# Two 32-row groups and held-back stores in a streaming RMSNorm + SiLU kernel

## The chip, the cores and the metric

The kernel runs on one core of one Trainium2 chip. The metric is the device time of one launch in microseconds. Before the change it is 160.66 us, the median of three runs that lie between 160.58 and 160.77 us. One further execution was taken with the hardware profiler: its own time was 160.9 us, and the span from its first to its last instruction was 159.4 us. The core has four engines that matter here (DVE, ACT, POOL and PE, the last of which only passes signals on), SP, whose queue issues the transfers, and 16 DMA engines that move the bytes between HBM and SBUF.

## The reference

```python
batch, seq, dim = 16, 1024, 512
x     = np.random.randn(batch, seq, dim).astype(np.float32)
gamma = np.ones(dim, dtype=np.float32)
eps   = np.float32(1e-5)

rms    = np.sqrt(np.mean(x ** 2, axis=-1, keepdims=True) + eps)
x_norm = x / rms * gamma
out    = x_norm * (1.0 / (1.0 + np.exp(-x_norm)))
```

There are 16,384 rows of 512 floats. Each row is normalised by its own root mean square, scaled by gamma and passed through SiLU. Every input byte is read once and every output byte is written once: 33.55 MB each way.

## The kernel before, in words

**Tiling.** Each of the 128 partitions of SBUF handles 128 rows ("rows" from here on means rows of a partition, 0 to 127; one such row is 2 KB for each partition and 256 KB over all of them). `groups` (line 28) says how the rows of a partition lie in HBM: a group of 16 rows covers 128 x 16 consecutive rows of the tensor, and partition p takes 16 consecutive ones of them, which are 32 KB in one piece. `dram` (line 105) turns a piece (first row, count) into that access pattern, and a piece may not cross a group's end. So a transfer of n rows has, for each partition, one contiguous run of n x 2 KB on both sides.

**The buffer.** `xb` holds `ring` = 96 rows a partition. Rows 96 to 127 reuse the places of rows 0 to 31, so those loads must wait until the stores of rows 0 to 31 have landed.

**The transfers.** `loads` and `stores` (lines 30 to 33) list the pieces, and `order` (lines 34 to 37) is the order in which SP issues them: eight loads (rows 0 to 95), then three stores (rows 0 to 31), then three loads (rows 96 to 127), then seven stores (rows 32 to 127). The first two loads are moved ahead of the start barrier (`early` = 2, lines 138 to 149). `load` (line 121) waits on the semaphore `st[u]` of a store whose place it overwrites; `store` (line 132) waits on `s_swish`, which counts finished units of compute. All of these transfers are on the one queue of SP, and SP works through them strictly in that order: a transfer that waits holds back everything listed behind it.

**The compute.** Work goes in units of `cn` = 4 rows, 32 units in all. PE waits for each load and adds its units to `s_land` (lines 156 to 159). ACT squares the four rows of a unit (`square`, line 184), DVE sums two of them (`sums`, line 211), POOL makes 1/sqrt (`power`, line 165), DVE multiplies each row by it and by gamma (`norm`, line 220), and ACT applies SiLU in place (`swish`, line 196) and counts `s_swish` up. ACT squares a unit two units before it applies SiLU (`lead` = 2).

Of the kernel before, what the change touches and what calls it, by code (L numbers as in the profile page):

```python
# [9 lines left out]
def kernel(  # L10
# [7 lines left out]
    nc = tc.nc  # L18
# [6 lines left out]
    of = out.flatten_outer_dims()  # L25
    R, D = xf.shape

    groups = [16] * 8
    ring = 96
    loads = [(0, 4), (4, 4), (8, 8), (16, 16), (32, 16), (48, 16), (64, 16), (80, 16)]  # L30
    loads += [(96, 16), (112, 8), (120, 8)]
    stores = [(0, 16), (16, 8), (24, 8), (32, 16), (48, 16), (64, 16), (80, 16)]
    stores += [(96, 16), (112, 8), (120, 8)]
    order = [("load", i) for i in range(loads.index((96, 16)))]
    order += [("store", t) for t in range(3)]
    order += [("load", i) for i in range(loads.index((96, 16)), len(loads))]
    order += [("store", t) for t in range(3, len(stores))]
    early = 2
    cn = 4
    n_sq = 2  # L40
# [46 lines left out]
    ld = [nc.alloc_semaphore(f"ld{t}") for t in range(len(loads))]  # L87
# [14 lines left out]
    def need(ins, sem, value):  # L102
        return ins.wait_op(sem, value, "sem-ge")

    def dram(ap, piece):
        a, n = piece
        g = max(g for g in range(len(groups)) if first[g] <= a)
        r = a - first[g]
        assert r + n <= groups[g], piece
        rows = ap[P * first[g] : P * (first[g] + groups[g])]  # L110
        return rows.rearrange("(p n) d -> p n d", n=groups[g])[:, r : r + n, :]

    def buf(piece):
        a, n = piece
        at = a % ring
        assert at + n <= ring, piece
        return xb[:, at : at + n, :]
# [3 lines left out]
    def load(i):  # L121
        a, n = loads[i]
        for u, (c, m) in enumerate(stores):
            over = c + ring < a + n and a < c + m + ring
            if over and u not in stored_by_sync:
                nc.sync.wait_ge(st[u], 16)
                stored_by_sync.add(u)
        return nc.sync.dma_start(
            out=buf(loads[i]), in_=dram(xf, loads[i])
        ).then_inc(ld[i], 16)  # L130

    def store(t):
        need(
            nc.sync.dma_start(out=dram(of, stores[t]), in_=buf(stores[t])),
            s_swish, ends[t],
        ).then_inc(st[t], 16)
# [11 lines left out]
        )  # L148
        entry.insert(at, ins)
    for what, t in order[early:]:  # L150
        load(t) if what == "load" else store(t)

    def take(queue, sem, n):
        need(queue.nop(nofuse=True), sem, n).then_inc(sem, -n)
# [151 lines left out]
```

## Time and profile before

| | |
|---|---|
| median of three runs | 160.66 us (160.58 to 160.77) |
| the profiled execution: time, span | 160.9 us, 159.4 us |
| ACT, DVE, POOL busy | 129.6, 124.5, 65.4 us |
| HBM read, written | 33.56 MB, 33.55 MB |
| ACT, after its first stalls | busy 99.71 of the 102.55 us from 37.95 to 140.50 us |
| last instruction of DVE, of ACT | about 138.5 and 140.5 us |
| last landing of a store | 159.3 us |

When SP issued each transfer and when its last byte was reported as landed (us from the start of the span, from the issue records and the semaphore updates):

| transfer (first row, rows) | issued | landed |
|---|---|---|
| loads (0,4) (4,4) (8,8) | 0.00, 0.43, 1.92 | 4.76, 7.24, 12.14 |
| loads (16,16) (32,16) (48,16) | 2.29, 2.77, 3.25 | 21.86, 31.57, 41.28 |
| loads (64,16) (80,16) | 3.88, 4.39 | 50.99, 61.62 |
| stores (0,16) (16,8) (24,8) | 30.09, 38.07, 46.05 | 71.29, 76.17, 81.19 |
| loads (96,16) (112,8) (120,8) | 71.31, 76.19, 81.20 | 90.76, 95.66, 100.56 |
| stores (32,16) (48,16) (64,16) | 81.58, 82.05, 93.95 | 110.44, 120.28, 130.15 |
| stores (80,16) (96,16) | 109.92, 125.88 | 139.92, 149.64 |
| stores (112,8) (120,8) | 133.87, 140.49 | 154.48, 159.33 |

Read the second table down its last column: the landings follow one another in the order of issue, and the column has no hole. Where a transfer was issued long before it landed, it stood in line behind the ones above it. From it four stages can be told apart: loads to about 61 us, stores to about 81 us, loads to about 100 us, stores to the end. The page's first two sections give the busy time of the compute engines and, in 40 slices of 4 us, how busy the 16 DMA engines were; its third section gives the number of packets. A packet is one contiguous run that one DMA engine moves: 8 KB for a piece of four rows, 16 KB for eight, 32 KB for sixteen. Each engine serves eight partitions, so it gets eight packets of every transfer, and a 4-byte packet that counts the semaphore up.

### The profile page before, as it was taken

What the parts mean: (1) busy time and instruction counts of PE and PEld (TensorE: products, weight loads), DVE (VectorE), ACT (ScalarE), POOL (GpSimd) and SP (SyncE); (2) the same over time, 40 slices, a digit from 0 to 9 for tenths busy, and PEclk for the clock granted to TensorE, in tenths of its full rate; (3) what the DMA queues carried; (4) which work ended last, traced back from release to release, by engine and by line L of the source; (5) the groups of instructions that cost most, each with busy time, mean ns of one, the idle gap of its engine ahead of it and who ended that gap; (6) DMA issues with size and microseconds to landing.
All of it is one profiled execution on the core that took longest, in us unless ns stands there. A gap on an engine that the chain in (4) does not pass through costs nothing. (4 is left out here: it accounts for less than half of the span.)

```text
span 159.4 us, 900 instructions
## 1 busy us (share of the span) xinstructions
DVE 124.5 (78%) x162; ACT 129.6 (81%) x193; POOL 65.4 (41%) x70
## 2 busy tenths in 40 slices
DVE  0187969999999999999999999999999999700000
ACT  0939959999999999999999999999999995720000
POOL 1052545555555555555555555555555555000000
DMA  7999999999999999999999999999999999999896
GB/s 267 454 465 395 452 469 395 411 502 403 395 469 452 395 395 395 395 399 448 415 448 469 391 432 428 485 428 395 469 444 403 403 493 411 411 469 436 382 419 259
DMA packets 3033, 67.12 MB, mean 421 GB/s; under 512 B 341, under 2 KB 341, under 8 KB 345
## 3 DMA queue, kind: packets, MB, share of 16 engines
q1 hardware_dynamic: 3024, 67.11, 98.8%
q10 hardware_dynamic: 8, 0.01, 0.0%
q14 instruction: 1, 0.00, 0.0%
HBM read 33.56 MB, written 33.55 MB: 421 GB/s over the span
## 5 line engine op out<-in xcount | busy, mean ns | idle before, releaser
L223 DVE SCALAR_TENSOR_TENSOR xb<-xb,rstd,gamma_sb 128x512 f32 (+1 forms) x128 | 87.3, 744 | 0.0
L198 ACT ACTIVATE xb<-xb (+1 forms) x32 | 60.9, 1902 | 2.8 <-DVE xb L223 2.8
L213 DVE TENSOR_REDUCE ms<-sq 128x2 f32<-128x1024 f32 x32 | 39.2, 1224 | 14.0 <-ACT sq L192 10.7
L168 POOL TENSOR_SCALAR aeps<-ms 128x4 f32<-128x4 f32 x32 | 20.6, 644 | 65.6 <-DVE ms L213 65.6
L175 POOL TENSOR_TENSOR rstd<-aeps,neg_half 128x4 f32<-128x4 f32 x32 | 44.1, 1377 | 2.7
L186 ACT ACTIVATE junk<-xb 128x512 f32 (+1 forms) x64 | 38.6, 603 | 4.5 <-PEq L159 4.4
L192 ACT ACTIVATE sq<-xb 128x1024 f32 (+1 forms) x32 | 32.1, 1005 | 0.0
L186 ACT ACTIVATION_READ_ACCUMULATOR junk<-xb 128x1 f32 x64 | 11.9, 186 | 0.0
L206 ACT ACT_TABLE_LOAD x1 | 1.3, 1283 | 3.6 <-issue 3.6
L161 POOL MEMSET gamma<- 128x512 f32 x1 | 0.5, 524 | 1.5 <-POOLq L71 1.5
L233 DVE STREAM_SHUFFLE gamma_sb<-gamma 128x512 f32<-128x512 f32 x1 | 0.7, 721 | 0.0
L287 POOL MEMSET const-float32-0.0<- 128x1 f32 x1 | 0.1, 98 | 0.2 <-issue 0.2
L287 POOL MEMSET const-bfloat16-1.0<- 128x1 bf16 x1 | 0.1, 101 | 0.0
L287 POOL MEMSET const-uint8-127<- 128x1 uint8 x1 | 0.1, 101 | 0.0
L162 POOL MEMSET neg_half<- 128x4 f32 x1 | 0.1, 101 | 0.0
L287 POOL MEMSET const-float32-1.0<- 128x1 f32 x1 | 0.1, 99 | 0.0
L233 DVE LOAD_MASK_SELECT gamma_sb<-gamma x1 | 0.0, 14 | 0.0
## 6 DMA issues: line engine op xcount, KB each, us to landing
xb<-in_x_dram SPq DMA_DIRECT2D x6, 4096.0 KB, 33.4
out_dram<-xb SPq DMA_DIRECT2D x6, 4096.0 KB, 33.1
out_dram<-xb SPq DMA_DIRECT2D x4, 2048.0 KB, 27.9
xb<-in_x_dram SPq DMA_DIRECT2D x3, 2048.0 KB, 19.4
xb<-in_x_dram SPq DMA_DIRECT2D x2, 1024.0 KB, 5.8
gamma<-in_gamma_dram ACTq DMA_DIRECT2D x1, 8.0 KB
```

What stands on the lines that cost most here:

```text
L161: nc.gpsimd.memset(gamma4, 0.0).then_inc(s_zero, 1)
L162: nc.gpsimd.memset(neg_half, -0.5).then_inc(s_half, 1)
L168: nc.gpsimd.tensor_scalar(out=aeps[:, m, :], in0=ms[:, m, :], scalar1=eps_f, scalar2=None, op0=ALU.add,),
L175: nc.gpsimd.tensor_tensor(out=rstd[:, m, :], in0=aeps[:, m, :], in1=neg_half, op=ALU.pow),
L186: acc = nc.scalar.activation(out=junk[(k % turn) * (cn - n_sq) + j - n_sq], in_=rows(at + j, 1)[:, 0, :], func=AF.Square, scale=inv_d**0.5 ...
L192: nc.scalar.activation(out=sq[k % turn], in_=rows(at, n_sq), func=AF.Square, scale=inv_d**0.5,).then_inc(s_sq, 1)
L198: nc.scalar.activation(out=rows(at, cn), in_=rows(at, cn), func=AF.Silu),
L206: nc.scalar.preload_act_table_set("silu_and_others")
L213: nc.vector.tensor_reduce(out=ms[:, k % turn, 0:n_sq], in_=sq[k % turn], op=ALU.add, axis=mybir.AxisListType.X,),
L223: ins = nc.vector.scalar_tensor_tensor(out=row, in0=row, scalar=rstd[:, k % turn, j : j + 1], in1=gamma_sb, op0=ALU.mult, op1=ALU.mult,)
L233: nc.vector.stream_shuffle(gamma_sb, gamma4, [0] * 32), s_gld, 16
L287: nc = _bacc.Bacc("TRN2", target_bir_lowering=False, num_devices=1)
```

## The change

Three things are different. The rows 32 to 63 and 64 to 95 become one group each of 32 rows, so a partition's run in HBM is 64 KB there. The pieces are cut anew: the first loading phase is (0,4) (4,4) (8,8) (16,16) (32,32) (64,28) (92,4), the second (96,16) (112,12) (124,4); the stores are (0,16) (16,16), and later (32,32) (64,32) (96,16) (112,8) (120,8). That makes 10 loads and 7 stores, where there were 11 and 10. And `order` has a third kind of entry, `landed`: ahead of each storing phase SP waits until the next to last load of the phase before has landed, which leaves the last load, four rows, in the queue. The compute code is the same.

```diff
-    groups = [16] * 8
+    groups = [16, 16, 32, 32, 16, 16]
     ring = 96
-    loads = [(0, 4), (4, 4), (8, 8), (16, 16), (32, 16), (48, 16), (64, 16), (80, 16)]
-    loads += [(96, 16), (112, 8), (120, 8)]
-    stores = [(0, 16), (16, 8), (24, 8), (32, 16), (48, 16), (64, 16), (80, 16)]
-    stores += [(96, 16), (112, 8), (120, 8)]
-    order = [("load", i) for i in range(loads.index((96, 16)))]
-    order += [("store", t) for t in range(3)]
-    order += [("load", i) for i in range(loads.index((96, 16)), len(loads))]
-    order += [("store", t) for t in range(3, len(stores))]
+    loads = [(0, 4), (4, 4), (8, 8), (16, 16), (32, 32), (64, 28), (92, 4)]
+    second = len(loads)
+    loads += [(96, 16), (112, 12), (124, 4)]
+    stores = [(0, 16), (16, 16)]
+    storing = len(stores)
+    stores += [(32, 32), (64, 32), (96, 16), (112, 8), (120, 8)]
+    order = [("load", i) for i in range(second)]
+    order += [("landed", loads.index((64, 28)))]
+    order += [("store", t) for t in range(storing)]
+    order += [("load", i) for i in range(second, len(loads))]
+    order += [("landed", loads.index((112, 12)))]
+    order += [("store", t) for t in range(storing, len(stores))]
...
     for what, t in order[early:]:
-        load(t) if what == "load" else store(t)
+        if what == "landed":
+            nc.sync.wait_ge(ld[t], 16)
+        else:
+            load(t) if what == "load" else store(t)
```

## The prediction

> **What bounds the kernel now.** I read the page's first two sections first, then the waits of SP's queue, then the DMA view cut into stretches small enough to hold packets of one size.
>
> ```profile
> span 159.4 us, 900 instructions
> DVE 124.5 (78%) x162; ACT 129.6 (81%) x193; POOL 65.4 (41%) x70
> ...
> DMA  7999999999999999999999999999999999999896
> ...
> q1 hardware_dynamic: 3024, 67.11, 98.8%
> ```
>
> No compute engine is busy for more than 81% of the span, while the 16 DMA engines are at 9 in every slice from the second to the 37th, and q1, SP's queue, has packets in flight for 98.8% of 16 engines' span: 157.5 us for each engine. So the time is the sum of the packets that one DMA engine must move, plus about 1 us until the first packet starts and about half a microsecond from the last to its report. An edit is worth what it does to the number or length of packets, or to a gap between them.
>
> ```profile
> SPq L134 <- ACT xb L198: 97.5, 9, 25.2
> SPq L128 <- DMA out_dram<-xb: 34.1, 3, 24.9
> SPq L270 <- DMA out_dram<-xb: 18.3, 3, 8.7
> ```
>
> SP waits for 97.5 us on compute (L134) and 34.1 us on stores whose places are to be reloaded (L128), yet no DMA slice falls under 9: there is always enough issued ahead. The shortest lead is that of the load of rows 96 on: the store it waits for landed at 71.29, it was issued at 71.31, and two 8-row stores (4.9 us each) were still queued.
>
> Then the packets. In each stretch, share x 16 x length / packets is the mean time of a packet. The four stretches, in order: 63 to 70 us (stores, 32 KB), 57 to 58 and 58 to 60 us (the last two packets of each engine's first loading phase, 32 KB), 96 to 99.4 us (the last loads of the second phase, 16 KB).
>
> ```profile
> DMA packets 96, 3.15 MB, mean 449 GB/s; under 512 B 0, under 2 KB 0, under 8 KB 0
> q1 hardware_dynamic: 96, 3.15, 104.0%
> ...
> DMA packets 16, 0.52 MB, mean 524 GB/s; under 512 B 0, under 2 KB 0, under 8 KB 0
> q1 hardware_dynamic: 16, 0.52, 147.2%
> ...
> DMA packets 16, 0.52 MB, mean 262 GB/s; under 512 B 0, under 2 KB 0, under 8 KB 0
> q1 hardware_dynamic: 16, 0.52, 100.9%
> ...
> DMA packets 92, 1.51 MB, mean 443 GB/s; under 512 B 0, under 2 KB 0, under 8 KB 0
> q1 hardware_dynamic: 92, 1.51, 103.4%
> ```
>
> A 32 KB packet takes 1.0400 x 16 x 7 / 96 = 1.213 us, a 16 KB one 1.034 x 16 x 3.4 / 92 = 0.611 us. But the last two load packets before the first stores take 1.472 and 2.018 us. This is the one place where all engines are slow together: (1.472 - 1.213) + (2.018 - 1.213) = 1.06 us for each engine. Before the second storing phase there is nothing of the kind: 0.611 us is the plain rate.
>
> **The change part by part.**
>
> *Fewer, larger packets.* Each engine gets eight packets of each transfer. Before, 21 transfers are 168 packets and 21 semaphore packets; after, 17 are 136 and 17. A packet's fixed part follows from the two sizes: 1.213 - 0.611 = 0.602 us is 16 KB, so 0.611 - 0.602 = 0.009 to 0.010 us are fixed. One engine's records overlap by 4 ns (32 KB starts stand 1.209 us apart), so 0.005 us is net. Saved: 36 x 0.005 = 0.18 us, at most 36 x 0.010 = 0.36 us. The trace has no 64 KB packet. From the line through 16 and 32 KB it is 2 x 1.204 + 0.010 = 2.417 us; were it split in two, it would cost 2 x 1.213 = 2.426, and the 24 split packets would give 24 x 0.005 = 0.12 back, leaving 0.06 us. I take 0.18, because the line is straight from 8 KB (0.311 us) on. Range of this term: 0 to -0.36 us.
>
> *Rows 32 on arrive later.* ACT squares row 32 at 37.95 us; its 16-row load landed at 31.57. The 32-row load lands with row 63, at about 41.28 as (48,16) did. ACT then stands still for 41.28 - 37.95 = 3.3 us; its chain ends at 143.8 instead of 140.5, since it is busy 99.71 of the remaining 102.55 us and can't catch up. Cover: the last store was issued at 140.49, while the store before it still had the DMA until about 154.0 us. 13 us of lead become 10. Tightest is the new store (64,32), which needs unit 24: ready at 109.92 + 3.3 = 113.3, while (32,32), 19.4 us long from about 100, keeps the engines to about 119. 6 us are left. Rows 64 to 91 land about 58, but ACT wants row 64 at 37.95 + 32 + 3.3 = 73. Cost: nothing; without the cover every microsecond of ACT's delay would count.
>
> *Fewer stores before the reload.* (16,8) and (24,8) become (16,16). The load (112,12) is then issued at about 81 rather than 76 us; ahead of it the load (96,16), 9.7 us, is in the queue. Cost: nothing.
>
> *The two waits.* Behind the waiting SP stand the stores, and behind those, in the first case, the loads from row 96 on, which wait for those stores anyway. At each wait four rows remain queued: 8 x (0.311 - 0.004) = 2.45 us an engine. In that time the semaphore must arrive, SP issue, and the first store packet start. Semaphore: the last 4-byte packet of store (0,16) starts at 70.93 us and its landing is at 71.29: 0.36 us. SP reacts in 0.02 us. From issue to first packet there is one row, the first load into empty engines: issued at 0.00, first packets from 1.02 to 1.55 us. Together 1.40 to 1.93 us, so 0.5 to 1.0 us is left on the slowest engine. The fastest ones are ahead by the spread of the semaphore packets, 0.46 us in the first phase (50.01 to 50.48) and 0.61 in the second (99.46 to 100.07): 0.1 us of hole at worst, on engines that don't end last. Cost: nothing; if the cover fails, the third case below.
>
> By the Trainium skill, page "DMA: Bandwidth & Descriptors", section "Latency and other measured facts", the same wait would be dearer: it gives an HBM access 2 us at high load and a first byte after about 0.6 us, together an estimate of 2.6 us, which is more than the four rows cover. By it each turn would stand dry for some 0.15 us, and the sum below would be about 0.3 us higher; the measured 0.36 us says that this core's queue is not in that state.
>
> *The slow turn at 57 to 61 us.* This decides the sign of anything measurable. Either the 1.06 us stays (bound 0) or the later issue and the 8 KB packets at the turn take it away (bound -1.06). No row shows a turn behind four rows. The nearest row is the second turn, at 100 us: there stores had been queued for 18 us as well (issued at 81.58), and it cost nothing. So early issue by itself is not what costs. What the second turn does not share with the first is that the first brings this run's first writes to the output, and that its load packets are of 32 KB. I take the first reading, a cost of the first stores, and 0.
>
> Sum: -0.18 + 0 + 0 + 0 + 0. On the profiled execution 160.9 (span 159.4 + 1.5) becomes 160.7; that execution stands 0.24 us above the median, so on the median 160.66 - 0.18 = 160.5 us.
>
> **The rivals.**
>
> *The slow turn goes.* For it: the excess falls exactly where stores follow loads, and 16 KB packets show none. Against it: the second turn is free with its stores queued early, and the slow packets come before any store packet has started. 160.48 - 1.06 = 159.4 us; a part of it left, in the ratio of 8 to 32 KB, gives 159.7.
>
> *The engines run dry at the turns.* It decides once the time from issue to first packet exceeds 2.45 - 0.38 = 2.07 us, against 1.02 to 1.55 at the start. Then the engines must be refilled: the 18 packets that start from 1.0 to 1.6 us take 1.263 x 16 x 0.6 / 18 = 0.67 us instead of 0.311, so 0.36 us a turn, and the hole comes on top, 0.48 us if a first packet needs 1 us more than at its slowest. Two turns: 160.48 + 0.72 = 161.2, with holes 162.2 us. For it: the margin is small and nothing shows the latency in a full queue. Against it: both known parts leave 0.5 us.
>
> *64 KB runs are not one packet, or are slower.* 160.6 us when split; a slower rate isn't suggested by any row.
>
> **How the numbers follow.** A measurement of this kernel can tell 0.2%, 0.32 us, from no change: 160.34 to 160.98. Forecast (turn stays, packets saved): 0.44, from 160.3 to 160.7, a quarter of it under 160.34. Turn goes: 0.33, all faster. Dry: 0.18, nearly all slower; larger runs that are slower: 0.05, slower. Faster 0.33 + 0.11 = 0.44, slower 0.23, the rest 0.33. The range goes from 159.2 (turn gone and 0.36 saved) to 161.3 (dry without much of a hole); the forecast's own is 160.3 to 160.7.
>
> **What would show it.** 136 + 17 packets an engine, 2.4 us for 64 KB; ACT idle for some 3 us before row 32 and its end near 144; DMA slices at 9 throughout; and in the stretch before the first stores either packets well above 0.311 and 1.213 us (turn stays) or none. A hole in the DMA row near 61 or 100 us, or a store packet that starts later than 2.07 us after its issue, would make the forecast wrong.

## The result, and the profile after

The changed kernel takes 159.92 us (median of six runs, 159.81 to 159.99) against 160.68 us before (six runs, 160.58 to 160.77). The ratio is 0.9949, with a 95% interval of 0.9939 to 0.9959: 0.76 to 0.82 us less, 0.5%. The profiled execution took 159.97 us with a span of 158.5 us.

The same lines of the page as were shown of before:

```profile
span 158.5 us, 896 instructions
DVE 124.5 (79%) x162; ACT 129.7 (82%) x193; POOL 65.4 (41%) x70
...
DMA  7999997989999969999999999896996996999996
...
q1 hardware_dynamic: 2448, 67.11, 98.6%
```

The compute engines are as busy as they were. There are 2448 packets instead of 3024, which is 16 engines x (136 + 17), and q1 has them in flight for 98.6% of a shorter span: 156.3 us for each engine instead of 157.5. The digits 6 to 8 in the DMA row are not holes. The row counts a packet's whole time in the slice in which it starts, and the packets of 56 and 64 KB take 2.1 and 2.4 us, so the slices of 4 us fill unevenly. By the packet records, an engine is without a packet for less than 0.1 us in all between 2 and 157 us, before and after.

Two stretches of the changed kernel's DMA view, from 57.7 to 59.7 us (the four rows held back ahead of the first stores, 8 KB packets) and from 102 to 116 us (stores of 64 KB runs):

```profile
DMA packets 98, 0.80 MB, mean 401 GB/s; under 512 B 0, under 2 KB 0, under 8 KB 0
q1 hardware_dynamic: 98, 0.80, 96.0%
...
DMA packets 92, 6.03 MB, mean 431 GB/s; under 512 B 0, under 2 KB 0, under 8 KB 0
q1 hardware_dynamic: 92, 6.03, 99.4%
```

By share x 16 x length / packets, the first are 0.960 x 16 x 2.0 / 98 = 0.313 us, the plain time of 8 KB: the slow packets ahead of the first stores are gone. The second are 0.994 x 16 x 14 / 92 = 2.42 us for 64 KB, one packet for each run; their records in the trace stand at 2.418 us.

Where the time went is read best from the landings at the end of each stage (issue plus time to landing, in the trace):

| | before | after | gained so far |
|---|---|---|---|
| rows 0 to 63 loaded | 41.28 | 41.18 | 0.10 |
| rows 0 to 95 loaded | 61.62 | 60.60 | 1.02 |
| rows 0 to 31 stored | 81.19 | 80.36 | 0.83 |
| rows 96 to 127 loaded | 100.56 | 99.74 | 0.82 |
| all stored | 159.33 | 158.43 | 0.90 |

The profiled execution before was 0.24 us above its median, so that 0.90 us here is a little more than the 0.76 us of the medians. Nearly the whole gain arises between 41 and 61 us, some 0.2 us of it is lost again by 80 us, and the rest is small. The loss is at the next turn, from stores back to loads, between 77.5 and 79.2 us of the changed kernel:

```profile
DMA packets 16, 0.52 MB, mean 308 GB/s; under 512 B 0, under 2 KB 0, under 8 KB 0
q1 hardware_dynamic: 16, 0.52, 81.9%
```

An engine's last store packet takes 0.819 x 16 x 1.7 / 16 = 1.39 us there on the mean instead of 1.213. Before the change the same turn was free; from 77 to 80 us a 16 KB packet took 1.007 x 16 x 3 / 79 = 0.612 us:

```profile
DMA packets 79, 1.29 MB, mean 431 GB/s; under 512 B 0, under 2 KB 0, under 8 KB 0
q1 hardware_dynamic: 79, 1.29, 100.7%
```

The two waits stand in the waits of SP's queue, at L156, as the longest ones. What SP waits for behind them is shorter than before, since it starts later:

```profile
SPq L156 <- DMA xb<-in_x_dram: 69.8, 2, 53.7
SPq L138 <- ACT xb L205: 45.1, 4, 15.6
SPq L132 <- DMA out_dram<-xb: 21.0, 2, 11.3
```

And the timeline of ACT has the stall at row 32, 3.28 us. Before the change ACT went on without one:

```profile
36.14 1.91 ACT L198 ACTIVATE xb<-xb  x1
37.95 0.61 ACT L186 ACTIVATE junk<-xb 128x512 f32 x1
```

And after:

```profile
36.10 1.91 ACT L205 ACTIVATE xb<-xb  x1
41.29 0.63 ACT L193 ACTIVATE junk<-xb 128x512 f32 x1 [3.28 <-PEq L166]
```

### The profile page after: what moved, and what is told of

It reads as the page before. It is cut to its first block, busy times and chain, and to the rows that moved or that the text cites. A ratio compares the mean times of both kernels' runs of the same rounds, so it can differ in the third digit from the quotient of the medians.

```text
span 158.5 us, 896 instructions
## 1 busy us (share of the span) xinstructions
DVE 124.5 (79%) x162; ACT 129.7 (82%) x193; POOL 65.4 (41%) x70
## 3 DMA queue, kind: packets, MB, share of 16 engines
q1 hardware_dynamic: 2448, 67.11, 98.6%
```

## The experiments

The DMA records give one number that all runs can be compared by: the time that packets took beyond the plain time of their size (0.309 us for 8 KB, 0.611 for 16, 0.912 for 24, 1.213 for 32, 2.116 for 56, 2.418 for 64), summed around a turn and divided by 16 engines. "Turn 1" is from loads to stores near 60 us, "turn 2" back to loads near 80, "turn 3" to stores near 100. "Held" means that SP issues what follows the turn only when four rows are left in the queue. Holes between packets are not in these numbers, and each is from the one execution that was traced, while the ratio is over all the runs. The runs were on several chips; each ratio is to the kernel before on the same chip, whose median lay between 160.67 and 160.81 us.

| kernel | turn 1 | turn 2 | turn 3 | ratio to before, 95% interval |
|---|---|---|---|---|
| before | 1.06 | 0 | 0 | |
| changed (1, 3 held) | 0.03 | 0.24 | 0 | 0.9949 (0.9939 to 0.9959) |
| changed, again | 0.03 | 0.26 | 0 | 0.9944 (0.9930 to 0.9959) |
| no waits | 1.11 | 0 | 0 | 1.0002 (0.9993 to 1.0012) |
| before, load cut | 0.72 | 0 | 0 | 1.0003 (0.9994 to 1.0012) |
| before, two waits, 16 rows left (8 at turn 3) | 1.04 | 0 | 0 | 1.0003 (0.9994 to 1.0012) |
| eight rows left | 1.19 | 0 | 0 | 1.0001 (0.9991 to 1.0011) |
| only turn 3 held | 1.23 | 0 | 0 | 1.0009 (0.9999 to 1.0018) |
| only turn 1 held | 0.03 | 0.49 | 0.86 | 1.0020 (0.9996 to 1.0043) |
| all three held | 0.03 | 0.53 | 0.02 | 0.9966 (0.9952 to 0.9980) |
| 16 KB stores before turn 2 | 0.03 | 0.44 | 0.03 | 0.9944 (0.9930 to 0.9957) |
| none left in the queue at 1, 3 | 0.05 | 0.81 | 0.05 | 1.0165 (1.0151 to 1.0178) |
| groups of 16, held | 0.03 | 0.25 | 0.08 | 0.9971 (0.9962 to 0.9980) |
| groups of 16, held, again | 0.03 | 0.33 | 0.08 | 0.9968 (0.9956 to 0.9981) |

### The new groups and pieces without the waits

```diff
-    order += [("landed", loads.index((64, 28)))]
-    order += [("landed", loads.index((112, 12)))]
```

> The changed kernel without its two waits: the 32-row groups and the new pieces stay, the stores are issued as soon as compute has them. Theory 'size' (the first turn is slow because the last load packets ahead of it are of 32 KB; four rows in 8 KB packets cure it): the turn stays free, 159.9 us as the changed kernel, ratio to before 0.995; 8 KB packets at 58 to 60 us at 0.31 us. Theory 'early' (stores that stand in the queue for a long time make the turn slow; the wait cures it): the turn is slow again by about 1 us, 160.6 to 160.9 us, ratio 1.000 to 1.001, with packets far over their plain time just ahead of the first store packets.

160.71 us: the whole gain is gone. From 57.75 to 60.5 us, the same four rows in 8 KB packets, now with stores queued behind them since 30 us:

```profile
DMA packets 81, 0.66 MB, mean 241 GB/s; under 512 B 0, under 2 KB 0, under 8 KB 0
q1 hardware_dynamic: 81, 0.66, 95.6%
```

They take 0.956 x 16 x 2.75 / 81 = 0.52 us instead of 0.31. So it isn't the size of the packets. The store packets start only after these, at 60.8 us; the loads ahead of them are what slows.

### The load cut, without waits

```diff
-(64, 16), (80, 16)]
+(64, 16), (80, 12), (92, 4)]
```

> The kernel before with one edit: load (80,16) is cut into (80,12) and (92,4), so that four rows in 8 KB packets stand ahead of the first stores; no waits, groups of 16. Theory 'size': the turn is free, minus 1.06 plus 9 packets at 0.005: 159.7 us, ratio 0.994. Theory 'early': stays slow, 160.7 us, ratio 1.000.

160.72 us, 0.72 us at turn 1. The small piece by itself does nothing for the time: the 0.72 is from an execution of 160.44 us, the fastest of eleven, so the difference to 1.06 can't be counted as a part of a cure. And "size" falls a second time, on the old kernel.

### The waits without the new pieces

```diff
+    order += [("landed", loads.index((64, 16)))]
     order += [("store", t) for t in range(3)]
...
+    order += [("landed", loads.index((112, 8)))]
     order += [("store", t) for t in range(3, len(stores))]
```

> The kernel before with the two waits alone: groups and pieces are as before, the first stores are issued when load (64,16) has landed (16 rows in 32 KB packets remain queued), the second stores when load (112,8) has landed. Theory 'early': issue comes 10 us ahead of the turn instead of 11 to 27, which should take most of the 1 us away: 159.7 to 160.1 us, ratio 0.994 to 0.997. Theory 'size': the 32 KB packets are there, so the turn stays slow: 160.7 us, ratio 1.000.

160.65 us, 1.04 us at turn 1. The first stores were issued at 51.09 us, ten microseconds ahead of the turn, where in the kernel before the three stood queued for 15 to 31 us, and the price is the same. From 57 to 60 us its last two load packets on each engine take 1.152 x 16 x 3 / 32 = 1.73 us on the mean instead of 1.213:

```profile
DMA packets 32, 1.05 MB, mean 350 GB/s; under 512 B 0, under 2 KB 0, under 8 KB 0
q1 hardware_dynamic: 32, 1.05, 115.2%
```

As "early" was put (the longer in the queue, the dearer) it fails as well.

### Eight rows left in the queue

```diff
-(64, 28), (92, 4)]
+(64, 24), (88, 8)]
...
-(112, 12), (124, 4)]
+(112, 8), (120, 8)]
```

> The changed kernel with eight rows left in the queue at each of the two waits instead of four: (64,24) (88,8) and (112,8) (120,8), so the stores are issued 4.9 us ahead of the turn and not 2.4. Theory 'queued well ahead' : between four rows (free) and sixteen (1.04 us at the first turn); if the price grows with the lead, about a third, 0.3 to 0.4 us at one turn, 160.3 us, ratio 0.9975. If it is an on-off matter with its point over 4.9 us: 159.9 us, 0.995; with its point under: about 1 us at the first turn, 160.7 us, 1.000.

160.83 us and the full price. The stores were issued at 55.75 us, and in the stretch from 57.5 to 59.9 us 16 KB packets take 0.963 x 16 x 2.4 / 36 = 1.03 us instead of 0.611:

```profile
DMA packets 36, 0.59 MB, mean 246 GB/s; under 512 B 0, under 2 KB 0, under 8 KB 0
q1 hardware_dynamic: 36, 0.59, 96.3%
```

So the price goes from nothing to full between the changed kernel and this one: the changed one issued at 58.20 us with its last load packets ending near 60.1, this one at 55.75 with an end that without the slowing would have been about the same. Nothing is paid with a lead of about 2 us, everything with about 4. Whether it is a step or a steep rise in between is not shown.

### No cover at all

```diff
-    order += [("landed", loads.index((64, 28)))]
+    order += [("landed", loads.index((92, 4)))]
...
-    order += [("landed", loads.index((112, 12)))]
+    order += [("landed", loads.index((124, 4)))]
```

> The changed kernel with the waits moved to the last load of each phase: nothing is queued while the semaphore, the issue and the first packet take their time. My price for a dry turn: 0.36 us to the landing, 0.02 to the issue, 1.02 to 1.55 us to the first packet, 0.36 us to refill: 1.8 to 2.3 us a turn, two turns: 159.9 + 3.5 to 4.6 = 163.4 to 164.5 us, ratio 1.017 to 1.024. If queued transfers start faster than the first load of the run did, less: under 1.01.

163.41 us, ratio 1.0165 (1.0151 to 1.0178): against the changed kernel's 0.9949 that is 0.0216 x 160.8 = 3.5 us. From 60 to 62 us, in 40 slices of 0.05 us (packets are counted where they start):

```profile
DMA  0000000000000000000000000000999900000000
DMA packets 25, 0.52 MB, mean 262 GB/s; under 512 B 9, under 2 KB 9, under 8 KB 9
q1 hardware_dynamic: 25, 0.52, 62.1%
```

From 60.2 to 61.4 us nothing starts. The stores were issued at 60.59, 0.08 after the landing, and the first packets of the 16 engines start from 61.43 to 61.58: 0.84 to 0.99 us from issue to packet. Four rows, 2.45 us, therefore cover the 0.36 + 0.08 + 0.99 = 1.4 us that a turn needs with a microsecond to spare.

By the packet records the slowest engine stands dry for 61.58 - 60.17 = 1.4 us at turn 1 and for 102.98 - 101.46 = 1.5 us at turn 3. Most of the other 0.6 us of the 3.5 is at turn 2, which pays 0.81 here instead of 0.24. There is no refill to pay: the first store packets take 1.24 us, where 1.213 is plain. So the expected sum came near the time partly by luck; it had a refill of 0.36 us a turn that did not occur, and not the price at turn 2 that did. The hold has a narrow place: too short and it costs about 1.5 us a turn, too long and it does nothing.

### One wait at a time

```diff
-    order += [("landed", loads.index((112, 12)))]
```

> The changed kernel with the wait ahead of the first stores alone; the second wait is taken out, so the stores from row 32 on are queued from about 81 us, some 16 us ahead of the turn at 98 us. Theory 'once' (only the first turn whose next transfers stand queued well ahead is slow; later ones are free, as in the kernel before): the store-to-load turn at 78 to 80 us has paid already, the turn at 98 us is free, 159.9 us, ratio to before 0.995. Theory 'every long-queued load-to-store turn pays' : 1 us more at 96 to 100 us, 160.7 us or more, ratio 1.000 to 1.002.

160.97 us, and turn 3, which was free in the kernel before with its stores queued 18 us ahead, now pays 0.86 us. From 97.75 to 99.7 us the 8 KB packets take 0.943 x 16 x 1.95 / 62 = 0.47 us:

```profile
DMA packets 62, 0.51 MB, mean 260 GB/s; under 512 B 0, under 2 KB 0, under 8 KB 0
q1 hardware_dynamic: 62, 0.51, 94.3%
```

The runs of this one scattered (160.19 to 162.31), and its interval reaches to 0.9996; the reading rests on the packets. The cleanest comparison is with the kernel that has neither wait: its stores from row 32 on were issued at 82.19 us, about as early as here (81.55), its pieces are the same, and its turn 3 is free. "Once" fails as it was put, since turn 2 had paid 0.49 and turn 3 paid again.

```diff
-    order += [("landed", loads.index((64, 28)))]
```

> The changed kernel with the wait ahead of the second storing phase alone. Both theories of the turn: the first turn is slow again, about 1 us, as without any wait: 160.6 to 160.7 us, ratio 0.999 to 1.000. If the second wait had a share of the gain, it would lie between 159.9 and 160.7 us.

160.95 us, 1.23 us at turn 1, nothing at the others. Neither wait is worth anything without the other: without the first, turn 1 pays; without the second, turn 3 does.

### Holding the loads as well

```diff
-    stores = [(0, 16), (16, 16)]
+    stores = [(0, 16), (16, 12), (28, 4)]
...
+    order += [("stored", 1)]
     order += [("load", i) for i in range(second, len(loads))]
...
+        elif what == "stored":
+            nc.sync.wait_ge(st[t], 16)
+            stored_by_sync.add(t)
```

> The changed kernel with the same hold at the turn from stores back to loads: the second store is cut into (16,12) and (28,4), and SP issues the loads from row 96 on when (16,12) has landed, with four rows of stores queued. Theory 'queued ahead' (what is queued long ahead of a change of direction slows the last packets before it, here 0.24 us an engine at 78 to 80 us): that goes, minus 0.24 plus 9 packets at 0.005: 159.7 us, ratio 0.9937. Theory 'once': the price moves to the next long-queued turn or is not paid at all, as every turn is now held: 159.7 us too. Theory 'store-to-load is slow by itself': 159.95 us, ratio 0.9952, the excess stays at 78 to 80 us. If the hold is too short for stores, whose landing is reported from HBM: a hole at 80 us, over 160.2 us.

160.13 us, a ratio of 0.9966 beside the changed kernel's 0.9949, so no better. The held-back store packets are at their plain time (0.309 us), but the price now falls on the loads: from 79.9 to 81.2 us fifteen 32 KB packets take 1.153 x 16 x 1.3 / 15 = 1.60 us each.

```profile
DMA packets 15, 0.49 MB, mean 378 GB/s; under 512 B 0, under 2 KB 0, under 8 KB 0
q1 hardware_dynamic: 15, 0.49, 115.3%
```

So the turn back to loads is not cured by holding. No version tried beats the changed kernel.

### Smaller stores ahead of turn 2

```diff
-    stores = [(0, 16), (16, 16)]
+    stores = [(0, 16), (16, 8), (24, 8)]
```

> The changed kernel with the store (16,16) cut into (16,8) and (24,8), as in the kernel before: the last stores ahead of the turn to loads are of 16 KB. Theory 'the turn from stores to loads pays when its packets are of 32 KB' (the kernel before, with 16 KB ones, shows nothing at 77 to 80 us): the 0.24 us go, 9 packets at 0.005 come, 159.7 us, ratio 0.994. Theory 'that turn pays because the one before it did not': the excess at 76 to 80 us stays, 159.95 us, 0.9952.

159.94 us, beside 159.93 of the changed kernel on the same chip; 0.44 us at turn 2. The packets' size is not the reason there either.

### The same with groups of 16

```diff
-    groups = [16, 16, 32, 32, 16, 16]
+    groups = [16] * 8
...
-(32, 32), (64, 28), (92, 4)]
+(32, 16), (48, 16), (64, 16), (80, 12), (92, 4)]
...
-(32, 32), (64, 32), (96, 16)
+(32, 16), (48, 16), (64, 16), (80, 16), (96, 16)
```

(The first wait is then on (80, 12).)

> The changed kernel with groups of 16 throughout: rows 32 to 95 go as (32,16) (48,16) (64,16) (80,12) (92,4) and are stored as four pieces of 16; both waits and the four rows ahead of each turn stay. Both theories of the turn: it stays free. Packets: 21 transfers instead of 17 are 36 more packets and semaphores an engine at 0.005 us, so 0.18 us over the changed kernel: 160.1 us, ratio to before 0.9964. If the 64 KB runs were worth nothing it is 159.9; if they were worth the whole gain, 160.7.

160.22 us. The rest of the changes, groups apart, give 0.0029 x 160.7 = 0.47 us. A second time, on one chip with the changed kernel:

> The changed kernel with groups of 16 throughout (36 more packets and semaphores an engine), on the same chip as the changed kernel. Theory 'count' (0.005 us each, as between 16 and 32 KB): 0.18 us over the changed kernel, ratio to before 0.9960 to 0.9965. Theory 'large runs do more than the count' (the earlier runs, on different chips, lie 0.0022 apart): 0.35 us over it, ratio 0.997. Theory 'nothing' (the same pieces and groups without waits gave nothing): the same as the changed kernel.

> The changed kernel once more, beside the others of this call on one chip: ratio to before 0.994 to 0.996; first turn free, about 0.25 us an engine of slow packets at 76 to 80 us, none at 95 to 100 us.

160.22 against 159.93 us: the 32-row groups are worth 0.29 us by the medians and (0.9968 - 0.9944) x 160.67 = 0.39 us by the ratios, whose intervals touch at their edges. The count of packets gives 0.18 us, at most 0.36. The runs don't tell "count" at its upper end from "more than the count"; "nothing" is unlikely with the waits in. The traces don't settle it: both executions traced with groups of 16 were slower than their median, and in both one engine ends its last load more than 1 us behind the middle engine at turn 3 (100.28 and 100.39 us against 99.16), where in the changed kernel the last is 0.3 us behind; the trace with 16 KB stores, which has the 32-row groups, shows the same lag. Without the waits, groups and pieces together gave 0.0002 in the wrong direction. In that trace rows 0 to 95 have landed at 61.77 us, 0.15 later than in the kernel before, which would take up most of the 0.18 us; why they do is not shown.

## Why the prediction was right and wrong

The measured time lies in the range, and "faster" was the likeliest of the three signs, but that is luck of a kind: 0.33 of the 0.44 for "faster" came from the first rival, and so did the low end of the range. The forecast itself, 160.5 us with 160.3 to 160.7 as its own range, was not what happened. The first rival was, with a part of its gain given back.

**What bounds the kernel**: right. The landings show 0.90 us of the 0.93 us between the two profiled executions, while the compute engines' busy times moved by 0.1 us at most. One of the signs given, DMA slices at 9 throughout, is not what the row shows, but the uneven digits come from the longer packets and not from holes.

**Packets**: the count and the 64 KB packet (2.418 us against 2.417 worked out) were right. The term, 0.18 us, was on the small side of 0.29 to 0.39 us, though its range of up to 0.36 reaches into that; the runs do not show that the count is the whole of it.

**Rows 32 on arrive later**: right in size, 3.28 us against 3.3, and in cost: the last store was issued at 143.85 us, while the store before it landed at 153.56.

**Fewer stores before the reload**: right that it costs nothing; the load (112,12) was issued at 80.37 us, while (96,16) was still on its way until 89.95, and with the two 8-row stores back the time was the same.

**The two waits**: right that the cover holds. The margin was 1.0 us, the upper end of the 0.5 to 1.0 I gave it, as a first packet follows its issue in 0.84 to 0.99 us in the run without cover and not in the 1.02 to 1.55 us of the run's first load. From the figures of the Trainium skill, page "DMA: Bandwidth & Descriptors", section "Latency and other measured facts", 2.6 us was the estimate for what the 2.45 us had to cover; in the run without cover it took about 1.4, and the changed kernel's turns show no hole. The refill of 0.36 us a turn, a term of the rival "the engines run dry", did not show either: 1.24 us for the first 32 KB packets after a hole.

**The slow turn**: this is the step that failed, in the sentence "I take the first reading, a cost of the first stores, and 0". The argument for it was that turn 3 was free with its stores queued as early. It was free, but not because queueing early is free: with turn 1 held and turn 3 not, turn 3 pays 0.86 us, and with neither held it pays nothing. In place of the 0 that the forecast put for the slow turn, 1.03 us went at turn 1 (1.06 before, 0.03 after). A stage that costs nothing had been read as a stage of the same kind as the one that costs, and what had gone before it, a turn that had paid, was left out. "A cost of the first stores" is refuted by the changed kernel, whose first stores come without it.

**The rival "slow turn goes"** said 159.4 us; 159.92 was measured. The 1.03 us at turn 1 did go, and 0.24 us came back at turn 2, which no case of mine had, because that turn was free before.

**What stays open**: why a load-to-store turn with stores queued about 4 us or more ahead slows the last three microseconds of loads, why it does so only until a load-to-store turn has paid once (in all six kernels where turn 1 paid, turn 2 was free, and so was turn 3 in the five of them that issued its stores 4 us or more ahead), and why the turn back to loads pays 0.24 to 0.81 us only where turn 1 was free. The runs show that packet size, the time in the queue beyond 4 us and the first use of the output are not the reason.

The page "DMA: Bandwidth & Descriptors" of the Trainium skill advises, under "Rules for kernel authors", to issue a DMA early and wait for it late when it is to overlap with compute, so that its fixed setup cost overlaps. At turn 1 of this kernel that holds only up to a point: issued 2 us ahead the stores cost nothing, 4 us ahead about 1 us.

## What to carry to other kernels

One kernel shows this, so it is something to try and not a rule. When reads and writes share one saturated queue, compute the mean packet time just ahead of each change of direction; packets above their plain time are a cost that no compute view shows. Then try issuing the far side of the turn late, with just more queued than semaphore, issue and first packet need (1.4 us here), and test all turns together, since curing one can move its price to the next. A stage that is free today is no proof that its pattern is free: here turn 3 was free only in kernels where turn 1 had paid or where its own stores were held.

## What the runs showed that was not expected

A wait that only delays an issue, with nothing else changed, made a saturated transfer stream faster: with the new pieces in place, 160.71 us without the two waits (ratio 1.0002) and 159.92 us with them (0.9949). And the effect is narrow: with 0, 4 and 8 rows left in the queue the kernel takes 163.41, 159.92 and 160.83 us, ratios of 1.0165, 0.9949 and 1.0001.
